# Final norm with the residual put into PSUM ahead of the last expert's rows, and a new order of low-row counts among the experts

## The chip, the cores and the metric

The kernel runs on one core of one Trainium2 chip. Five engines work side by side, each through its own queue of instructions: TensorE (PE, matrix products into PSUM), VectorE (DVE), ScalarE (ACT), GpSimd (POOL, also the issuer of gathers and scatters) and SyncE (SP, the issuer of plain DMA). They meet at semaphores. The metric is the device time of one execution in microseconds, the median of several runs.

## The reference

One decoder layer on 1024 tokens of width 1024: token mixers, cross-attention, then a hierarchical mixture of experts and a final norm. The change touches the last two.

```python
# per token: best of 4 groups, best 2 of that group's 4 experts, weights `combine` (n, 16)
a = einsum("nd,edf->nef", hf, w_gate);  b = einsum("nd,edf->nef", hf, w_up)
u = silu(a) * b * combine[..., None]
y = einsum("nef,efd->nd", u, w_down)
x = x + y
out = x * rsqrt(mean(x * x, -1) + 1e-6) * norm_final_g
```

## The kernel before

**The experts.** Each of the 16 experts gets its routed tokens as slots: 128 slots in a first part (h = 0) and, where it has more tokens, a second part of low rows (h = 1). Experts 0 and 1 run early. The other 14 are sorted by token count at run time, and `RANKS` says which rank runs at which place, so it fixes how many low rows a place has room for: ranks 0 to 3 have 64, ranks 4 to 9 have 32, ranks 10 to 13 none. Places are numbered by e = 2 to 15; e = 15 is `LAST` and has no low rows. In the loop over e the rows of expert e+1 are gathered (`fetch`, L1294, GpSimd), transposed (`turn`, L1240 for the 128 rows, L1304 for low rows), expert e's gate and up products run (`early`, L141 to L143, three passes hi·hi, hi·lo, lo·hi), then `store_low(e)` (L1376), `gate_up_low(e+1)` (L1359), and `store(e, 0)`: `down` in two halves of 512 columns, scaled on ScalarE into `yt` (L1323) and added to the rows of `xo_dram` by an indirect DMA from GpSimd (L1341). An addition waits for all additions of the expert before; within one expert the low one is issued first.

**The end.** `xo_dram` then holds the residual with all experts but `LAST`. Its eight row tiles (128 tokens by 1024) come back as `x3[0]` to `x3[7]` by eight loads on SP (L1530), which wait for expert 14's additions. `last_rows` runs `down` for `LAST`; each half is split into a high and a low part (`yl[0]` on ScalarE, L133, `yl[1]` on VectorE, L137). `mine` holds, for each row tile, a 128 by 128 selection matrix; two products with it (hi and lo) for each half put `LAST`'s rows at their tokens ("selection products"). For a tile in `ON_PE` (1, 3, 5, 7) a PSUM tile of two banks gets the selection products and then the residual, by a product of `ident` with `x3[t]` (L1565). For the others `last_add` lets VectorE add PSUM to `x3[t]` half by half (L1552). ScalarE squares and sums a tile (L1566 or L1570), takes the root (L1572), VectorE makes the factor `r` by four small instructions (L1573 to L1576). Then the tile is scaled: by VectorE from PSUM with `gfin` in one pass (L1581), or GpSimd has multiplied `x3[t]` with `gfin` (L1571) and ScalarE (L1585) or VectorE (tile 6, L1583) applies `r`. SP stores the tile (L1586).

The order of the instructions in each queue is made ahead of time by a scheduler from the order in the code and its own costs; on the chip each queue runs as it was written.

Of the kernel before, what the change touches and what calls it, by code (L numbers as in the profile page):

```python
# [12 lines left out]
AF = mybir.ActivationFunctionType  # L13
OP = mybir.AluOpType
AX = mybir.AxisListType

P = 128
D = 1024
T = 1024
KD = 8  # L20
NT = 8
# [7 lines left out]
SLOTS = 2 * P  # L29
LOW = 64  # L30
EARLY = 2
ON_PE = (1, 3, 5, 7,)
ON_V = (6,)
YTS = 2
XTS = 2
QT = 2
# [2 lines left out]
SQP = (1, 3, 5, 7)  # L39
LAST = NE - 1  # L40
NS = NE - EARLY
RANKS = [0, 10, 1, 11, 2, 12, 3, 4, 5, 6, 7, 8, 9, 13]
R64, R32 = 4, 10
DR = 0
LOWS = {EARLY + i: LOW if r < R64 else LOW // 2 if r < R32 else 0 for i, r in enumerate(RANKS)}
# [9 lines left out]
def half(n):  # L55
    return slice(n * HALF, n * HALF + HALF)


def blk(i):
    return slice(i * P, i * P + P)  # L60
# [3 lines left out]
def layer_kernel(ctx, tc, a, out, dbg=None):  # L64
    nc = tc.nc
    dbg = dbg or {}
    V, A, G, TE = nc.vector, nc.scalar, nc.gpsimd, nc.tensor
# [18 lines left out]
    @contextmanager  # L86
    def psum(**tags):
        with tc.tile_pool(name="psum", bufs=1, space=bass.MemoryType.PSUM, reuse_waits="tile") as p:
            banks.update(pool=p, tags=tags)
            yield  # L90

    def bank(tag, shape=None):
        return banks["pool"].tile(shape or [P, HALF], F32, name="ps_" + tag, tag=tag, bufs=banks["tags"][tag])

    pstack = ctx.enter_context(ExitStack())
# [7 lines left out]
    ident = consts.tile([P, P], F32, name="ident")  # L103
# [95 lines left out]
    r = hpool.tile([P, T], F32, name="r")  # L199
# [1040 lines left out]
                TE.transpose(pt[:, k], xg[:, blk(4 * b + k)], ident)  # L1240
            split(hi[:, 4 * b:4 * b + 4], lo[:, 4 * b:4 * b + 4], pt)

    def down(u_, dn, evac):
        for n in range(2):
            ps = bank("lin")
            for f in range(2):
                mm3(ps, (u_[0][:, f], u_[1][:, f]), (dn[0][f][:, half(n)], dn[1][f][:, half(n)]),
                    f == 0, f == 1)
            evac(half(n), ps)
# [282 lines left out]
    def last_rows():  # L1532

        idf = ro.tile([P, NT], F32, name="idf", tag="idf", bufs=1)
        mine = xt_p.tile([P, T], F32R, name="mine", tag="xt1b", bufs=2)
        for t in range(NT):
            V.tensor_scalar(idf[:, t:t + 1], sids[:, 0, LAST:NE], float(-t * P), None, op0=OP.add)
            V.tensor_scalar(mine[:, blk(t)], place[:, :P], idf[:, t:t + 1], None, op0=OP.is_equal)
        yl = [hxp.tile([P, D], F32R, name=f"yl{i}", tag=f"h2{i}", bufs=4) for i in range(2)]

        def evac(ns, ps):
            split(yl[0][:, ns], yl[1][:, ns], ps, scale=slots_of(LAST, 0)[:, 0, LAST:NE])

        down(U[LAST, 0], W[LAST][1], evac)
        return mine, yl

    def last_add(t):
        for n in range(2):
            ps = bank("lin")
            for i in range(2):  # L1550
                TE.matmul(ps, mine[:, blk(t)], yl[i][:, half(n)], start=i == 0, stop=i == 1)
            V.tensor_tensor(x3[t][:, half(n)], x3[t][:, half(n)], ps, op=OP.add)  # L1552

    room = [(wst, "w_hi"), (wst, "w_lo"), (wst, "w_raw"), (exg, "xg")]

    def row_sums(t):

        ss, v, r, tmp = (ro.tile([P, 1], F32, name="f" + c, tag="f" + c + "1", bufs=3) for c in "svrt")
        o = room[t // 2][0].tile([P, D], F32, name="of", tag=room[t // 2][1], bufs=2)
        if t in ON_PE:  # L1560
            x = bank("pair", [P, D])
            for n in range(2):
                for i in range(2):
                    TE.matmul(x[:, half(n)], mine[:, blk(t)], yl[i][:, half(n)], start=i == 0, stop=False)
                TE.matmul(x[:, half(n)], ident, x3[t][:, half(n)], start=False, stop=True)  # L1565
            A.activation(o, x, AF.Square, scale=0.5 * D ** -0.5, accum_out=ss)  # L1566
        else:
            last_add(t)
            x = ex.tile([P, D], F32, name="sq", tag="yt", bufs=YTS)
            A.activation(x, x3[t], AF.Square, scale=0.5 * D ** -0.5, accum_out=ss)  # L1570
            G.tensor_tensor(o, x3[t], gfin, op=OP.mult)  # L1571
        A.activation(r, ss, AF.Sqrt, bias=eps4)  # L1572
        V.tensor_scalar(v, ss, EPS / 4, None, op0=OP.add)  # L1573
        V.reciprocal(tmp, r)
        V.tensor_scalar(tmp, v, tmp, r, op0=OP.mult, op1=OP.add)
        V.reciprocal(r, tmp)  # L1576
        return t, o, x, r

    def row_out(t, o, x, r):
        if t in ON_PE:  # L1580
            V.scalar_tensor_tensor(o, x, r, gfin, op0=OP.mult, op1=OP.mult)  # L1581
        elif t in ON_V:
            V.tensor_scalar(o, o, r, None, op0=OP.mult)  # L1583
        else:
            A.activation(o, o, AF.Copy, scale=r)  # L1585
        nc.sync.dma_start(out[blk(t)], o)  # L1586

    early(LAST, 0)
# [1 line left out]
    with tc.issue_after(order["split"].ins):  # L1590
        A.activation(warm, eps, AF.Sqrt)
    pstack.close()
    pstack.enter_context(psum(lin=2, pair=3))
    mine, yl = last_rows()
    pend = []
    for t in range(NT):
        pend.append(row_sums(t))
        if t >= 1:
            row_out(*pend.pop(0))
    for x in pend:  # L1600
# [5 lines left out]
    pstack.close()  # L1606
    nover = nc.values_load(cnt[0:1, 0:1], min_val=0, max_val=T)
    with tc.If(nover > 0), psum(lin=2, tra=2, acc=1, pair=1):
        for t in ON_PE:
            last_add(t)  # L1610
        with tc.tile_pool(name="ov", bufs=1) as op_:
            with tc.For_i(0, NE, 1) as e:
                more = nc.values_load(excess[0:1, bass.ds(e, 1)], min_val=0, max_val=T)
                with tc.If(more > 0):
                    gu = gu_weights(a["w_gu"][bass.ds(e, 1)].rearrange("o p k n -> p (o k) n"),
                                    lambda i, b: op_.tile([P, 2, HALF], F32R, name=f"gu2{i}", tag=f"gu2{i}", bufs=4))
                    dn = dn_weights(a["w_dn"][bass.ds(e, 1)].rearrange("o p k n -> p (o k) n"))
                    ow = op_.tile([P, NT], F32, name="ow2")
                    nc.sync.dma_start(ow, ov_dram[:, bass.ds(e, 1)].rearrange("p o t -> p (o t)"))
                    xh = [op_.tile([P, KD, P], F32R, name=f"xh{i}") for i in range(2)]  # L1620
                    uo = [op_.tile([P, 2, P], F32R, name=f"uo{i}") for i in range(2)]
                    for t in range(NT):
                        xg = op_.tile([P, D], F32, name="xg2", tag="xg2", bufs=2)
                        nc.sync.dma_start(xg, h3_dram[blk(t)])
                        rows_in(xg, *xh)

                        def evac(ns, ps, t=t):
                            V.scalar_tensor_tensor(x3[t][:, ns], ps, ow[:, t:t + 1], x3[t][:, ns],
                                                   op0=OP.mult, op1=OP.add)

                        gate_up_t(op_, *xh, gu, *uo)
                        down(uo, dn, evac)
        with tc.tile_pool(name="fin2", bufs=1) as fn:
            for t in range(0, NT, 2):
                scaled(*sums(fn, t, 2))
# [77 lines left out]
```

## Time and profile before

| | us |
|---|---|
| median of 3 runs (1232.41 to 1239.38) | 1232.83 |
| the profiled execution | 1231.35 |
| its span, first to last instruction | 1229.5 |
| start of the residual loads | 1201.07 |
| first square of the final norm | 1208.02 |
| end of the last VectorE pass of the final norm | 1223.63 |

TensorE is busy 94% of the span, VectorE 68%, ScalarE 51%, GpSimd 33%; the granted TensorE clock is 0.988 in the mean. The times of the rows count from the span's start; what lies around the span is 1231.35 - 1229.5 = 1.85 us. In the page and the trace, "idle before" names what ended an engine's wait.

### The profile page before, as it was taken

The numbers are of one execution on the slowest core, as the hardware profiler recorded it, in microseconds if no ns is written. First come the engines' busy times: TensorE is split into PE (matmuls) and PEld (weight loads), VectorE is DVE, ScalarE is ACT, GpSimd is POOL, SyncE is SP. The second block draws the span as 40 slices with busy tenths as digits, with TensorE's granted clock in tenths as the row PEclk, the third lists the DMA queues.
The fourth block names the chain that finished last, engine by engine and source line by source line (L and its number), as shares of the span: only waits on it lengthen the run. The fifth ranks groups of instructions, "written<-read, shape, count | busy, mean of one in ns | idle before, by whom it ended". The sixth has DMA issues, their size and how long they took to land. (4 is left out here: it accounts for less than half of the span.)

```text
span 1229.5 us, 17120 instructions
## 1 busy us (share of the span) xinstructions
PE 1158.4 (94%) x6173; PEld 908.2 (74%) x6174; DVE 840.8 (68%) x1569; ACT 629.5 (51%) x1059; POOL 403.2 (33%) x276
## 2 busy tenths in 40 slices
PE   7999999999999999999999999999997798999995
PEld 3778887778877777788888787787764676667773
DVE  5499997653978788791235853655988885766665
ACT  6345564521655555482333343643752575767765
POOL 4328995301010110101011665264015122233343
PEclk9999999999999999999999999999998899999999
DMA  5211224126211111111344443244257889999967
GB/s 208 76 47 40 75 80 167 40 86 231 71 59 41 45 58 47 39 46 54 103 149 142 154 158 112 66 121 122 78 196 249 282 243 303 311 284 314 314 170 285
DMA packets 57468, 174.12 MB, mean 142 GB/s; under 512 B 7993, under 2 KB 11081, under 8 KB 57377
## 3 DMA queue, kind: packets, MB, share of 16 engines
q1 hardware_dynamic: 49680, 149.76, 36.1%
q0 software_dynamic: 7696, 23.20, 8.0%
q8 instruction: 51, 0.84, 0.3%
q14 instruction: 41, 0.33, 0.1%
HBM read 136.92 MB, written 36.01 MB: 141 GB/s over the span
## 5 line engine op out<-in xcount | busy, mean ns | idle before, releaser
L135 POOL TENSOR_TENSOR w_lo<-w_raw,w_hi 128x1024 fp32r<-128x1024 f32 x58 | 140.2, 2417 | 474.7 <-ACT w_hi L133 464.9
L143 PE MATMUL ps_lin<-hh,w_lo 128*128 128x512 f32 x560 | 222.5, 397 | 2.3 <-POOL w_lo L135 2.2
L141 PE MATMUL ps_lin<-hh,w_hi 128*128 128x512 f32 x560 | 222.9, 398 | 0.7 <-DVE u L355 0.6
L142 PE MATMUL ps_lin<-hl,w_hi 128*128 128x512 f32 x560 | 221.7, 396 | 0.0
L133 ACT ACTIVATE w_hi<-w_raw 128x1024 fp32r<-128x1024 f32 (+1 forms) x100 | 92.1, 921 | 201.2 <-PE ps_lin L142 161.0
L143 PEld LDWEIGHTS ps_lin<-hh,w_lo 128*128 128x128 f32 x560 | 105.6, 189 | 25.0 <-POOL w_lo L135 4.4
L141 PEld LDWEIGHTS ps_lin<-hh,w_hi 128*128 128x128 f32 x560 | 105.7, 189 | 23.6 <-issue 3.4
L142 PEld LDWEIGHTS ps_lin<-hl,w_hi 128*128 128x128 f32 x560 | 105.6, 189 | 21.3 <-issue 1.3
L377 DVE SCALAR_TENSOR_TENSOR ps_cva<-u,dw_w,ps_cva 128x1024 f32<-128x1024 f32 x90 | 111.6, 1279 | 0.5
L137 DVE SCALAR_TENSOR_TENSOR gu<-e_raw,gu 128x1024 fp32r<-128x1024 f32 x64 | 77.5, 1222 | 4.7 <-ACT gu L133 1.0
L373 POOL TENSOR_TENSOR oc<-oc,pj 128x512 f32<-128x512 f32 x60 | 76.0, 1323 | 8.8 <-ACT pj L372 8.7
L133 ACT ACTIVATE gu<-e_raw 128x1024 fp32r<-128x1024 f32 x64 | 67.4, 1058 | 8.9 <-PE ps_lin L143 7.4
L141 PE MATMUL ps_lin<-gu,xgT 128*128 128x512 f32 x144 | 58.3, 405 | 4.1 <-ACT xgT L133 4.1
L372 ACT ACTIVATE pj<-u,dw_w 128x512 f32<-128x512 f32 x60 | 42.4, 721 | 34.3 <-POOL oc L373 34.2
L137 DVE SCALAR_TENSOR_TENSOR dn<-d_raw,dn 128x1024 fp32r<-128x1024 f32 x32 | 39.1, 1227 | 27.8 <-ACT dn L133 27.7
L557 ACT ACTIVATE sc<-sc,mns 128x128 f32<-128x128 f32 (+3 forms) x64 | 49.4, 773 | 15.6 <-DVE mns L553 15.2
L142 PE MATMUL ps_lin<-gu,xgT 128*128 128x512 f32 x144 | 56.9, 395 | 0.0
L143 PE MATMUL ps_lin<-gu,xgT 128*128 128x512 f32 x144 | 56.6, 393 | 0.0
L1294 POOL DMA_INDIRECT xg<-h_dram,ids x29 | 34.3, 1183 | 66.2 <-PE ps_sco L1070 23.3
L137 DVE SCALAR_TENSOR_TENSOR pl<-ps_tra,ph 128x512 fp32r<-128x512 f32 (+1 forms) x80 | 49.1, 636 | 9.3 <-ACT ph L133 8.2
L133 ACT ACTIVATE ph<-ps_tra 128x512 fp32r<-128x512 f32 (+1 forms) x80 | 41.7, 552 | 23.3 <-PE ps_tra L570 22.5
L570 PE MATMUL ps_tra<-ident,sc 128*128 128x128 f32 x288 | 47.5, 274 | 4.2 <-DVE sc L560 4.2
(471 smaller groups left out, 2850.4 us busy)
## 6 DMA issues: line engine op xcount, KB each, us to landing
e_raw<-in_w_gu SPq DMA_DIRECT2D x64, 512.0 KB, 6.8
w_raw<-in_w_in SPq DMA_DIRECT2D x36, 512.0 KB, 3.8
d_raw<-in_w_dn SPq DMA_DIRECT2D x32, 512.0 KB, 9.5
w_raw<-in_w_out SPq DMA_DIRECT2D x16, 512.0 KB, 3.5
xT<-in_xT SPq DMA_DIRECT2D x16, 256.0 KB, 5.4
gc_dram<-gc SPq DMA_DIRECT2D x8, 512.0 KB, 4.2
gc<-gc_dram SPq DMA_DIRECT2D x8, 512.0 KB, 4.0
mc_dram<-gc SPq DMA_DIRECT2D x8, 512.0 KB, 2.9
```

Of the source, the lines that this page charges most:

```text
L133: order["split"] = A.activation(hi, src, AF.Copy, scale=scale)
L135: G.tensor_tensor(lo, src, hi.bitcast(F32), op=OP.subtract)
L137: V.scalar_tensor_tensor(lo, src, scale, hi.bitcast(F32), op0=OP.mult, op1=OP.subtract)
L141: TE.matmul(ps, lh, rh, start=first, stop=False)
L142: TE.matmul(ps, lh, rl, start=False, stop=False)
L143: return TE.matmul(ps, ll, rh, start=False, stop=last)
L372: A.activation(pj, uj, AF.Copy, scale=dw_h[:, c, j:j + 1])
L373: G.tensor_tensor(co[c][:, ns], co[c][:, ns], pj, op=OP.add)
L377: V.scalar_tensor_tensor(sums, u[c][:, j:j + T], dw_h[:, c, j:j + 1], sums, op0=OP.mult, op1=OP.add)
L557: A.activation(sc[:, :nk], sc[:, :nk], AF.Exp, scale=-1.0, bias=mns[:, nch - 1:nch], accum_out=sm)
L570: TE.transpose(pt[:, s_], pr[i][:, blk(j)], ident)
L1294: G.indirect_dma_start(out=XG[e, h][:n], out_offset=None, in_=src, in_offset=bass.IndirectOffsetOnAxis(ap=idx, axis=0))
```

## The change

It has two parts. In the final norm, seven of the eight tiles are now summed in PSUM (all but tile 2, `BY_ADD`), in a ring of four two-bank tiles that also holds `LAST`'s `down`. `residual(t)` puts `ident` times `x3[t]` into the tile first, two tiles ahead of the selection products. Tiles 1 and 4 (`BY_ACT`) are scaled with `r` by ScalarE out of PSUM and then multiplied with `gfin` by GpSimd; tile 2 goes by GpSimd and VectorE as tile 6 did; tiles 0, 3, 5, 6 and 7 are scaled by VectorE in one pass, the last one in two halves, each stored by itself. In `RANKS`, rank 12 moves from place 7 to place 14: place 14 loses its 32 low rows, place 7 gets 64, place 8 has 32 in place of 64, and the sum of all stays (four times 64, six times 32).

```diff
-ON_PE = (1, 3, 5, 7,)
-ON_V = (6,)
+BY_ADD = (2,)
+BY_ACT = (1, 4)
-RANKS = [0, 10, 1, 11, 2, 12, 3, 4, 5, 6, 7, 8, 9, 13]
+RANKS = [0, 10, 1, 11, 2, 3, 4, 5, 6, 7, 8, 9, 12, 13]
...
-        down(U[LAST, 0], W[LAST][1], evac)
+        ps = bank("pair", [P, D])
+        down(U[LAST, 0], W[LAST][1], evac, lambda n: ps[:, half(n)])
...
+    def residual(t):
+        if t < NT:
+            SUM[t] = bank("pair", [P, D])
+            if t not in BY_ADD:
+                for n in range(2):
+                    TE.matmul(SUM[t][:, half(n)], ident, x3[t][:, half(n)], start=True, stop=False)
...
     def row_sums(t):
...
-            last_add(t)
+        if t in BY_ADD:
+            last_add(t, SUM[t])
...
+        else:
+            x = SUM[t]
+            for n in range(2):
+                last_rows_of(x[:, half(n)], t, n, False)
+            A.activation(o, x, AF.Square, scale=0.5 * D ** -0.5, accum_out=ss)
...
     def row_out(t, o, x, r):
+        if t in BY_ADD:
+            V.tensor_scalar(o, o, r, None, op0=OP.mult)
+        elif t in BY_ACT:
+            A.activation(o, x, AF.Copy, scale=r)
+            G.tensor_tensor(o, o, gfin, op=OP.mult)
+        elif t == NT - 1:
+            for n in range(2):
+                V.scalar_tensor_tensor(o[:, half(n)], x[:, half(n)], r, gfin[:, half(n)], op0=OP.mult, op1=OP.mult)
+                nc.sync.dma_start(out[blk(t), half(n)], o[:, half(n)])
+            return
+        else:
             V.scalar_tensor_tensor(o, x, r, gfin, op0=OP.mult, op1=OP.mult)
...
-    pstack.enter_context(psum(lin=2, pair=3))
+    pstack.enter_context(psum(pair=4))
     mine, yl = last_rows()
     pend = []
+    residual(0)
+    residual(1)
     for t in range(NT):
         pend.append(row_sums(t))
+        residual(t + 2)
         if t >= 1:
             row_out(*pend.pop(0))
```

TensorE at the start of the final norm, before: the end of `LAST`'s `down` (`dn`, `uh`, `ul`), then selection products (`yl`, `mine`), and the first residual (tile 1, `x3r_11254`) after five of them.

```order
L141 MATMUL ps_lin_11338<-dn0_11200,uh_11268 128x512
L142 MATMUL ps_lin_11338<-dn1_11201,uh_11268 128x512
L143 MATMUL ps_lin_11338<-dn0_11200,ul_11269 128x512
L1564 MATMUL ps_pair_11373<-yl0_11327,mine_11310 128x512
L1564 MATMUL ps_pair_11416<-yl0_11327,mine_11310 128x512
L1551 MATMUL ps_lin_11352<-yl0_11327,mine_11310 128x512
L1551 MATMUL ps_lin_11352<-yl1_11328,mine_11310 128x512
L1564 MATMUL ps_pair_11373<-yl1_11328,mine_11310 128x512
L1565 MATMUL ps_pair_11373<-x3r_11254,ident_77 128x512
```

The same place now: `ps_pair_11329` is `down`'s tile, `11346` and `11349` are tiles 0 and 1 (line numbers of rows "now" are those of the changed kernel).

```order
L143 MATMUL ps_pair_11329<-dn0_11212,ul_11269 128x512
L1566 MATMUL ps_pair_11346<-x3r_11252,ident_77 128x512 x2
L141 MATMUL ps_pair_11329<-dn0_11208,uh_11268 128x512
L142 MATMUL ps_pair_11329<-dn1_11209,uh_11268 128x512
L143 MATMUL ps_pair_11329<-dn0_11208,ul_11269 128x512
L141 MATMUL ps_pair_11329<-dn0_11212,uh_11268 128x512
L142 MATMUL ps_pair_11329<-dn1_11213,uh_11268 128x512
L143 MATMUL ps_pair_11329<-dn0_11212,ul_11269 128x512
L1566 MATMUL ps_pair_11349<-x3r_11254,ident_77 128x512 x2
L1550 MATMUL ps_pair_11346<-yl0_11327,mine_11310 128x512
L1550 MATMUL ps_pair_11346<-yl1_11328,mine_11310 128x512
```

The residual of tile 0, which reads the loaded `x3r_11252`, now stands between the two halves of `down`, that of tile 1 behind the second half, and all selection products behind both.

VectorE at the first two tiles, before (`fs`, `fr` and `ft` are the sums, the factor `r` and a help tile; L1576 writes `r`):

```order
L1574 RECIPROCAL ft_11350<-fr_11349 128x1
L1573 TENSOR_SCALAR fv_11369<-fs_11368 128x1
L1574 RECIPROCAL ft_11371<-fr_11370 128x1
L1575 TENSOR_SCALAR ft_11350<-fv_11348,ft_11350,fr_11349 128x1
L1575 TENSOR_SCALAR ft_11371<-fv_11369,ft_11371,fr_11370 128x1
L1576 RECIPROCAL fr_11349<-ft_11350 128x1
L1576 RECIPROCAL fr_11370<-ft_11371 128x1
L1581 SCALAR_TENSOR_TENSOR of_11372<-ps_pair_11373,fr_11370,gfin_11248 128x1024
```

The same place now (L1586 writes `r`; `11354` belongs to tile 0, `11370` to tile 1, `x3r_11256` is tile 2):

```order
L1584 RECIPROCAL ft_11355<-fr_11354 128x1
L1585 TENSOR_SCALAR ft_11355<-fv_11353,ft_11355,fr_11354 128x1
L1584 RECIPROCAL ft_11371<-fr_11370 128x1
L1586 RECIPROCAL fr_11354<-ft_11355 128x1
L1585 TENSOR_SCALAR ft_11371<-fv_11369,ft_11371,fr_11370 128x1
L1601 SCALAR_TENSOR_TENSOR of_11356<-ps_pair_11346,fr_11354,gfin_11248 128x1024
L1586 RECIPROCAL fr_11370<-ft_11371 128x1
L1555 TENSOR_TENSOR x3r_11256<-x3r_11256,ps_pair_11367 128x512 x2
```

The pass of tile 0 (L1601, 1024 columns) now stands ahead of tile 1's `r`, and the two additions of tile 2 behind both.

ScalarE from the first square on, now (L1581 and L1575 square, L1582 roots, L1593 scales tile 1 from PSUM):

```order
L1581 ACTIVATE of_11356,fs_11352<-ps_pair_11346 128x1024
L1581 ACTIVATE of_11372,fs_11368<-ps_pair_11349 128x1024
L1582 ACTIVATE fr_11354<-fs_11352,eps4_11250 128x1
L1582 ACTIVATE fr_11370<-fs_11368,eps4_11250 128x1
L1593 ACTIVATE of_11372<-ps_pair_11349,fr_11370 128x1024
L1575 ACTIVATE sq_11399,fs_11388<-x3r_11256 128x1024
L1581 ACTIVATE of_11417,fs_11413<-ps_pair_11383 128x1024
```

ScalarE's scaling of tile 1 stands ahead of the squares of tiles 2 and 3.

## Rows read from the trace of the kernel before

**Rows 1.** Busy time by stretch, the final norm and what follows (columns: first line)

```profile
core 0: us, PE busy (x) PEld busy (x) DVE busy (x) ACT busy (x) POOL busy (x), PEclk, DMA share, GB/s
...
1205.70:1223.60 17.90, 13.35 (x43) 7.95 (x43) 14.39 (x45) 13.23 (x27) 9.56 (x4) 0.99 0.88 352
...
1223.60:1229.50 5.90, 0.00 (x0) 0.00 (x0) 0.04 (x1) 0.00 (x0) 0.00 (x0) 0.50 0.39 157
```

**Rows 2.** Waits of the SP queue from 1150; the residual loads, line L1530

```profile
SPq L1530 <- DMA xo_dram<-yt,sids: 35.3, 1, 35.3
...
L1530 SPq DMA_DIRECT2D x3r<-xo_dram x8: 331/384/402, 1201.1 to 1204.4; - x8
...
DMA to landing us min/median/max: 3.3/7.3/10.0
```

**Rows 3.** Timeline of TensorE (start, duration, instruction, idle before and its releaser)

```profile
1200.58 0.50 PE L141 MATMUL ps_lin<-dn,uh 128*128 128x512 f32 x1 [0.47 <-ACT uh L133]
...
1203.22 0.39 PE L143 MATMUL ps_lin<-dn,ul 128*128 128x512 f32 x1
...
1205.68 1.12 PE L1565 MATMUL ps_pair<-x3r,ident 128*128 128x512 f32 x2 [0.90 <-DMA x3r<-xo_dram]
...
1206.24 1.03 PE L1551 MATMUL ps_lin<-yl,mine 128*128 128x512 f32 x2
...
1209.35 0.39 PE L1564 MATMUL ps_pair<-yl,mine 128*128 128x512 f32 x1
...
1212.68 0.62 PE L1564 MATMUL ps_pair<-yl,mine 128*128 128x512 f32 x2
```

**Rows 4.** Timeline of ScalarE, then of VectorE, in the same stretch

```profile
1202.28 0.69 ACT L133 ACTIVATE yl<-ps_lin,wsl 128x512 fp32r<-128x512 f32 x1 [0.24 <-PE ps_lin L143]
...
1208.02 1.06 ACT L1570 ACTIVATE sq<-x3r 128x1024 f32<-128x1024 f32 x1 [3.69 <-DVE x3r L1552]
...
1204.37 0.75 DVE L137 SCALAR_TENSOR_TENSOR yl<-ps_lin,wsl,yl 128x512 fp32r<-128x512 f32 x1 [0.62 <-ACT yl L133]
...
1205.04 0.68 DVE L1552 TENSOR_TENSOR x3r<-x3r,ps_lin 128x512 f32<-128x512 f32 x1
...
1211.33 1.28 DVE L1581 SCALAR_TENSOR_TENSOR of<-ps_pair,fr,gfin 128x1024 f32<-128x1024 f32 x1
...
1222.35 1.28 DVE L1581 SCALAR_TENSOR_TENSOR of<-ps_pair,fr,gfin 128x1024 f32<-128x1024 f32 x1
```

**Rows 5.** Groups of instructions, 1204 to 1224: count | busy, mean ns | idle

```profile
L1571 POOL TENSOR_TENSOR of<-x3r,gfin 128x1024 f32<-128x1024 f32 x4 | 9.6, 2389 | 14.1 <-DVE x3r L1552 14.1
...
L1566 ACT ACTIVATE of<-ps_pair 128x1024 f32<-128x1024 f32 x4 | 4.0, 1003 | 0.0
...
L1585 ACT ACTIVATE of<-of,fr 128x1024 f32<-128x1024 f32 x3 | 3.4, 1136 | 0.0
...
L1583 DVE TENSOR_SCALAR of<-of,fr 128x1024 f32<-128x1024 f32 x1 | 0.8, 752 | 0.1
```

**Rows 6.** Timeline of GpSimd's queue, expert 14's two additions

```profile
1192.85 1.57 POOL L1341 DMA_INDIRECT xo_dram<-yt,sids_low  x1 [6.23 <-ACT yt L1323]
...
1194.72 1.56 POOL L1341 DMA_INDIRECT xo_dram<-yt,sids  x1 [0.30 <-issue]
```

**Rows 7.** Timeline of ScalarE, expert 14's second half of yt

```profile
1193.34 0.69 ACT L1323 ACTIVATE yt<-ps_lin,wsl 128x512 f32<-128x512 f32 x1 [0.67 <-PE ps_lin L143]
```

**Rows 8.** Timeline of TensorE, end of gate and up of expert 14

```profile
1187.91 0.39 PE L143 MATMUL ps_lin<-gu,xgT 128*128 128x512 f32 x1
...
1188.23 1.07 PE L1376 MATMUL ps_sco<-d_raw,uL 128*32 128x256 f32 x16
...
1190.30 0.48 PE L141 MATMUL ps_lin<-dn,uh 128*128 128x512 f32 x1
```

**Rows 9.** The output stores, line L1586

```profile
DMA to landing us min/median/max: 3.2/3.8/4.4
```

**Rows 10.** Waits of TensorE from 985 to 1205: total, times, longest

```profile
PE ps_tra L1240 <- DMA xg<-h_dram,ids: 6.2, 3, 4.9
```

More of the change, by code (lines that the diff above doesn't have):

```diff
@@ L1241, in rows_in, with down @@
             split(hi[:, 4 * b:4 * b + 4], lo[:, 4 * b:4 * b + 4], pt)
-    def down(u_, dn, evac):
+    def down(u_, dn, evac, dst=lambda n: bank("lin")):
         for n in range(2):
-            ps = bank("lin")
+            ps = dst(n)
             for f in range(2):
@@ L1542, in evac, with last_rows_of, last_add @@
             split(yl[0][:, ns], yl[1][:, ns], ps, scale=slots_of(LAST, 0)[:, 0, LAST:NE])
-        down(U[LAST, 0], W[LAST][1], evac)
+        ps = bank("pair", [P, D])
+        down(U[LAST, 0], W[LAST][1], evac, lambda n: ps[:, half(n)])
         return mine, yl
-    def last_add(t):
+    def last_rows_of(ps, t, n, first):
+        for i in range(2):
+            TE.matmul(ps, mine[:, blk(t)], yl[i][:, half(n)], start=first and i == 0, stop=i == 1)
+    def last_add(t, ps):
         for n in range(2):
[L1549 to L1552, printed above, removed]
+            last_rows_of(ps[:, half(n)], t, n, True)
+            V.tensor_tensor(x3[t][:, half(n)], x3[t][:, half(n)], ps[:, half(n)], op=OP.add)
     room = [(wst, "w_hi"), (wst, "w_lo"), (wst, "w_raw"), (exg, "xg")]
+    SUM = {}
+    def residual(t):
[4 more added lines that the diff above has]
+                    TE.matmul(SUM[t][:, half(n)], ident, x3[t][:, half(n)], start=True, stop=False)
     def row_sums(t):
@@ L1559, in row_sums @@
         o = room[t // 2][0].tile([P, D], F32, name="of", tag=room[t // 2][1], bufs=2)
[L1560 to L1567, printed above, removed]
-            last_add(t)
+        if t in BY_ADD:
+            last_add(t, SUM[t])
             x = ex.tile([P, D], F32, name="sq", tag="yt", bufs=YTS)
@@ L1579, in row_out @@
     def row_out(t, o, x, r):
-        if t in ON_PE:
+        if t in BY_ADD:
[9 more added lines that the diff above has]
+        else:
             V.scalar_tensor_tensor(o, x, r, gfin, op0=OP.mult, op1=OP.mult)
[L1582 to L1585, printed above, removed]
         nc.sync.dma_start(out[blk(t)], o)
@@ L1608, in layer_kernel @@
     with tc.If(nover > 0), psum(lin=2, tra=2, acc=1, pair=1):
-        for t in ON_PE:
-            last_add(t)
+        for t in range(NT):
+            if t not in BY_ADD:
+                last_add(t, bank("pair", [P, D]))
         with tc.tile_pool(name="ov", bufs=1) as op_:
```

## Prediction

> **What bounds the kernel now.** TensorE is busy 94% of the span, but the change works where that no longer holds, so I read the end by stretches first. In the final norm, 1205.7 to 1223.6, TensorE is busy 13.35 of 17.9 us, VectorE 14.39, ScalarE 13.23, and the DMA engines 88% [rows 1]. No engine is full; what counts is the order in which they wait for each other. After 1223.6 nothing computes: 5.9 us for the last store and the end of the program.
>
> Second, what starts the stretch. The SP queue waits for expert 14's additions and issues the eight loads of `x3` from 1201.07 on; the quickest takes 3.3 us, the last issued (1204.4) cannot take more than 10.0, so the tiles land from about 1204.4 to 1214.4 [rows 2]. TensorE has finished `LAST`'s `down` by then (12 products from 1200.58, the last started at 1203.22, so 0.23 us apiece) and first meets a load at the residual of tile 1, where it stands 0.90 us [rows 3]. The first square begins at 1208.02, the last VectorE pass ends at 1222.35 + 1.28 = 1223.63 [rows 4].
>
> So the load of `x3[0]` is the gate. VectorE read that tile at 1205.04 [rows 4], and 1201.07 + 3.3 = 1204.4 is the earliest; I take 1204.4. Today everything that waits for no load runs ahead of it: all of `down`, both splits, five selection products. What was left from 1204.4 to 1223.63 is 19.2 us.
>
> **The change, part by part: the norm.** I walk the new order from 1204.4, with durations of before.
>
> 1. TensorE now has the residual of tile 0 between the two halves of `down`. Its price: from 1209.35 to 1212.68 before, TensorE ran the two residual halves of tile 3 with its last three selection products, and tile 4's four [rows 3]. 3.33 - 7 x 0.23 = 1.72, so 0.86 per half and 1.72 per tile. It ends at 1206.1.
> 2. The second half of `down` follows, 6 x 0.23 = 1.4: 1207.5. (It also waits for VectorE's split of the first half, because both halves now lie in one tile; the ScalarE split began at 1202.28 and took 0.69 [rows 4], VectorE's takes 0.75, so this is over long before.)
> 3. The residual of tile 1, 1.72: 1209.2. Under it ScalarE and VectorE split the second half (0.69 + 0.75 from 1207.6: 1209.05), so the split costs nothing; without the cover it would cost 1.4.
> 4. Four selection products of tile 0 and their drain, 0.92 + 0.15: first square at 1210.3. Before: 1208.02.
> 5. Two squares, two roots, the four small VectorE steps. Before, from the first square to the scaling pass: 1208.02 to 1211.33, 3.3 us [rows 4]; now tile 1's `r` is not in between, so 3.1: the pass of tile 0 starts at 1213.4 and ends, after 1.28, at 1214.7.
> 6. Only then does VectorE make tile 1's `r` (0.15), and ScalarE's next instruction is the scaling of tile 1 with that `r`. Behind it in ScalarE's queue stand the squares of tiles 2 and 3, and the square of tile 2 also needs two VectorE additions that stand behind the pass. From the roots (about 1212.8) to 1214.85 ScalarE waits, some 2 us. Scaling from PSUM has no row; squaring from PSUM takes 1.003, scaling from SBUF 1.136 [rows 5]. I take 1.05: 1215.9.
> 7. GpSimd multiplies tile 1 by `gfin`, then makes tile 2's product; 2.389 each [rows 5]: 1220.7. VectorE's scaling of tile 2 waits for the second, 0.75 [rows 5]: 1221.4. Tile 3's `r` and pass stand behind it in VectorE's queue: 0.15 + 1.28, 1222.85.
> 8. Tile 7's residual needs the PSUM tile that this pass frees (a ring of four: `down`, 0, 1, 2, then 3 in `down`'s place, ..., 7 in tile 3's). In TensorE's queue it stands ahead of tile 6's selection products. 1.72 + 1.07: 1225.65. Tiles 4 and 5 and GpSimd's third product run beside this.
> 9. Squares of 6 and 7 to the pass of tile 6, as in step 5, 3.1; the pass, 1.28: 1230.0. Tile 7's `r` and two half passes, 0.15 + 2 x 0.68 (a VectorE addition of 512 columns took 0.68 [rows 4]): 1231.5.
>
> That is 27.1 us in place of 19.2: +7.9. What is saved, one ScalarE scaling (1.14) and three of the four tiles of VectorE additions (six of 0.68), lies beside this chain.
>
> The last store is half as large. 256 KB less at the stretch's 352 GB/s is 0.7 us; the bounds are nothing and 0.75. I take 0.7: +7.2.
>
> **The change: the order of low rows.** Expert 14's additions were two, issued at 1192.85 and 1194.72 [rows 6]; the first goes. The second needs `yt`, whose second half ends at 1193.34 + 0.69 = 1194.03 [rows 7], so it can gain 0.7 at most. Against that, `store_low(14)`, 1.07 us on TensorE, stood between the end of gate and up (1187.91) and `down` (1190.30) [rows 8] and covered the way from there through silu to `uh`. Without it eight transposes (1.0) remain as cover, and TensorE waits for up to 0.9 us. The addition and so the loads move by -0.7 to +0.2; I take 0. Place 7 gets 64 low rows and place 8 loses 32, the sum over all places stays, so I take 0 for the loop too.
>
> At one place of this walk everything hangs on TensorE not passing a product that waits. The trace shows it: VectorE's split ended at 1204.37 + 0.75 = 1205.12, but the selection products of tile 0 that needed only it are recorded at 1206.24, behind the residual that waited until 1205.68 [rows 3, 4]. The Trainium skill ("PSUM — Partial Sum Buffer", section "Engine vs sequencer instructions") says that matmuls start and complete in program order and that the queues of the other three engines are strict first-in first-out. If products could pass, steps 1 and 3 would leave the path and the sum would be 3.4 lower, +3.8; the trace agrees with the rule.
>
> For the half store the Trainium skill ("DMA: Bandwidth & Descriptors", section "Anatomy of one DMA — SWDGE (gpsimd) path") gives a fit of about 2.0 us plus bytes over 436 GB/s for another way of issuing. By it 512 KB take 3.2, which is the shortest of the eight stores here [rows 9], and 256 KB an estimated 2.6; the sum would be +7.3.
>
> **The rivals.**
>
> *Shorter: the residuals lie in time that TensorE had idle.* If `x3[0]` and `x3[1]` landed before the first half of `down` is through (1200.58 + 1.4 = 1202.0), steps 1 to 4 would cost little, and with one scaling less on ScalarE (1.14), half a store (0.7) and half a pass (0.64) the end would come 2.5 earlier: 1230.3. For it: TensorE does stand idle there. Against it: the loads would have to land 2.4 us earlier and the removed addition gives 0.7 at most; and steps 6 to 8 stay.
>
> *Half the loss.* Steps 6 to 8 hold 10.9 us, in which waits of three engines follow each other without a gap in my walk. If GpSimd's product or ScalarE's scaling is quicker than I take them, or the loads come 0.7 earlier, the sum falls by some 3 to 5: 1236.
>
> *More: the loop loses too.* Gathers of `xg` stand behind a low addition in GpSimd's queue, and that waits for all additions of the expert before. TensorE waited 6.2 us for gathered rows in three places, 4.9 in one [rows 10]. A second run of 64 low rows behind a first (places 6 and 7) could make one more such wait: +4.9, 1245. Against it: with 32 rows, six such places in a row cost the other two waits only, 1.3 us.
>
> **How the numbers follow.** The sum is made against the profiled execution: span 1229.5 + 7.2 = 1236.7, time 1231.35 + 7.2 = 1238.55. The median of the runs is 1232.83, 1.5 above it; on it the same sum gives 1240.0, the predicted time. Chances: the walk as it stands, 1237 to 1243, 0.66; half the loss, 0.15; more, 0.10; shorter, 0.07; anything else 0.02. The range 1235 to 1245 takes in the first, most of the second and half of the third; it leaves out the shorter one. About 1% (12.3 us) is what a measurement of this kernel can tell from no change: slower by more needs 1245.2, half of the third case, 0.06; faster by more has no case, 0.01; within 1%, 0.93.
>
> **What would show it.** Right: TensorE waits for a load behind six products of `down`; the first square about 2.3 us later; ScalarE idle for about 2 us before it scales tile 1; two GpSimd products back to back, and VectorE's tile 2 waiting for the second; the last VectorE pass near 1231.5. Wrong: a first square by 1208.5, loads issued by 1199, or a TensorE wait for `xg` at place 7 or 8.

## The result, and the profile after

The changed kernel takes 1246.4 us (median of 9 runs, 1238.69 to 1247.81) where the kernel before, over 9 runs of its own, takes 1236.46 (1232.41 to 1240.13): a ratio of 1.0076 with an interval of 1.0059 to 1.0092, so 7.3 to 11.4 us slower. The forecast was 1240.0 in a range of 1235 to 1245. The direction was right and the size was not: the range was left by 1.4 us.

| | before | changed |
|---|---|---|
| median of the runs, us | 1236.46 (the first three runs: 1232.83) | 1246.4 |
| span of the profiled execution, us | 1229.5 | 1244.4 |
| first product of `LAST`'s `down` to the end of the last VectorE pass, us | 23.05 | 30.91 |
| that end to the end of the span, us | 5.87 | 5.56 |

The two spans differ by 14.9 us, which is more than the medians do (9.9). Of the 14.9, 3.9 lie ahead of expert 13's low `down` products, 3.4 in a stretch of lower clock behind a wait at the end of the expert loop, and 7.9 in the norm; the last store gives 0.3 back. The experiments below take up each.

First the final norm. Timeline of TensorE in the changed kernel (start, duration, instruction, idle time before and its releaser), the rows that answer to [rows 3]:

```profile
1209.20 0.39 PE L143 MATMUL ps_pair<-dn,ul 128*128 128x512 f32 x1
1211.18 1.98 PE L1566 MATMUL ps_pair<-x3r,ident 128*128 128x512 f32 x4 [1.60 <-DMA x3r<-xo_dram]
1212.60 0.79 PE L141 MATMUL ps_pair<-dn,uh 128*128 128x512 f32 x1
...
1214.38 1.88 PE L1566 MATMUL ps_pair<-x3r,ident 128*128 128x512 f32 x4
1215.70 2.39 PE L1550 MATMUL ps_pair<-yl,mine 128*128 128x512 f32 x8
...
1229.88 1.95 PE L1566 MATMUL ps_pair<-x3r,ident 128*128 128x512 f32 x4 [0.49 <-PE ps_pair L1550]
```

TensorE has done the sixth product of `down` and stands 1.60 us for `x3[0]`; the other six wait behind that residual, and the residual of tile 1 stands ahead of the selection products of tile 0. Each residual has four records, two for each half. ScalarE, GpSimd and VectorE in the same stretch, which answer to [rows 4, 5]:

```profile
1217.22 1.02 ACT L1581 ACTIVATE of<-ps_pair 128x1024 f32<-128x1024 f32 x1 [1.95 <-PE ps_pair L1550]
...
1221.71 1.11 ACT L1593 ACTIVATE of<-ps_pair,fr 128x1024 f32<-128x1024 f32 x1 [2.01 <-DVE fr L1586]
...
1222.91 2.36 POOL L1594 TENSOR_TENSOR of<-of,gfin 128x1024 f32<-128x1024 f32 x1 [20.11 <-ACT of L1593]
1225.23 2.37 POOL L1576 TENSOR_TENSOR of<-x3r,gfin 128x1024 f32<-128x1024 f32 x1
...
1210.34 0.75 DVE L137 SCALAR_TENSOR_TENSOR yl<-ps_pair,wsl,yl 128x512 fp32r<-128x512 f32 x1 [2.01 <-ACT yl L133]
...
1220.33 1.28 DVE L1601 SCALAR_TENSOR_TENSOR of<-ps_pair,fr,gfin 128x1024 f32<-128x1024 f32 x1
...
1227.64 0.75 DVE L1591 TENSOR_SCALAR of<-of,fr 128x1024 f32<-128x1024 f32 x1 [0.41 <-POOL of L1576]
...
1228.50 1.28 DVE L1601 SCALAR_TENSOR_TENSOR of<-ps_pair,fr,gfin 128x1024 f32<-128x1024 f32 x1
...
1237.43 1.41 DVE L1597 SCALAR_TENSOR_TENSOR of<-ps_pair,fr,gfin 128x512 f32<-128x512 f32 x2
```

ScalarE stands 2.01 us before it scales tile 1, GpSimd makes two products back to back, VectorE's tile 2 waits for the second. Then the end of the expert loop, which the forecast put down as worth nothing. TensorE and GpSimd there:

```profile
1192.67 1.06 PE L1240 MATMUL ps_tra<-ident,xg 128*128 128x128 f32 x8 [1.96 <-DMA xg<-h_dram,ids]
...
1194.75 0.79 PE L141 MATMUL ps_lin<-dn,uh 128*128 128x512 f32 x1 [0.80 <-ACT uh L133]
...
1186.38 1.57 POOL L1341 DMA_INDIRECT xo_dram<-yt,sids_low  x1 [8.87 <-DVE dn L137]
1188.26 1.00 POOL L1294 DMA_INDIRECT xg<-h_dram,ids  x1 [0.30 <-PE ps_lin L143]
...
1201.23 1.57 POOL L1341 DMA_INDIRECT xo_dram<-yt,sids  x1 [9.78 <-ACT yt L1323]
```

The last gather of `xg` is issued at 1188.26, behind expert 13's low addition, and TensorE stands 1.96 us for its rows and another 0.80 for `uh`. Neither wait is there before. Busy time by stretch, with the granted clock in the third column from the end:

```profile
core 0: us, PE busy (x) PEld busy (x) DVE busy (x) ACT busy (x) POOL busy (x), PEclk, DMA share, GB/s
...
1195.00:1200.00 5.00, 5.00 (x12) 3.87 (x13) 1.76 (x8) 0.69 (x1) 0.00 (x0) 0.50 0.09 17
...
1211.18:1238.84 27.66, 21.53 (x66) 12.21 (x66) 14.12 (x42) 13.00 (x27) 7.09 (x3) 0.99 0.62 249
1238.84:1244.40 5.56, 0.00 (x0) 0.00 (x0) 0.00 (x1) 0.00 (x0) 0.00 (x0) 0.50 0.38 144
```

Behind those waits the granted clock is 0.50, that is 1.2 of 2.4 GHz, from about 1194 to 1201. The norm has grown to 27.66 us, 21.53 of them with TensorE busy; in [rows 1] it was 13.35 of 17.9.

### The profile page after: what moved, and what is told of

It reads as the page before. It is cut to its first block, busy times and chain, and to the rows that moved or that the text cites. A ratio compares the mean times of both kernels' runs of the same rounds, so it can differ in the third digit from the quotient of the medians.

```text
span 1244.4 us, 17142 instructions
## 1 busy us (share of the span) xinstructions
PE 1170.1 (94%) x6185; PEld 914.2 (73%) x6186; DVE 839.7 (67%) x1565; ACT 628.4 (50%) x1058; POOL 402.6 (32%) x275
```

## The experiments

All kernels compute the whole result. The table holds four stretches of every profiled execution; a ratio is of several runs, with its interval, and three rows are of a single execution. S is the start of expert 13's low `down` products (L1376), D the first product of `LAST`'s `down`, V the end of the last VectorE pass; each is read from the timelines as above (before: S is 1174.31, D and V are 1200.58 and 1222.35 + 1.28 in [rows 3, 4]).

| kernel | start to S | S to D | D to V | V to end | ratio to before |
|---|---|---|---|---|---|
| before | 1174.31 | 26.27 | 23.05 | 5.87 | |
| before, again | 1174.58 | 26.30 | 22.49 | 5.83 | one execution |
| old norm, new order (`ranks_only`) | 1181.93 | 26.06 | 22.76 | 5.75 | 1.0037 (1.0008 to 1.0065) |
| new norm, old order (`norm_only`) | 1178.34 | 26.28 | 30.80 | 5.38 | 1.0060 (1.0037 to 1.0083) |
| changed | 1178.23 | 29.70 | 30.91 | 5.56 | 1.0076 (1.0059 to 1.0092) |
| changed, again | 1183.10 | 26.30 | 30.66 | 5.64 | one execution |
| changed, whole last store | 1183.02 | 31.60 | 30.21 | 5.87 | one execution |
| residuals behind `down` | 1175.71 | 26.10 | 28.09 | 5.50 | 1.0039 (1.0014 to 1.0065) |
| the same, old order | 1175.88 | 26.27 | 28.47 | 5.48 | 1.0025 (0.9995 to 1.0054) |
| the same, new order, no ScalarE scaling | 1181.28 | 26.08 | 28.32 | 5.42 | 1.0064 (1.0037 to 1.0090) |
| changed, unread rows gone | 1174.85 | 23.51 | 33.95 | 5.49 | 1.0048 (1.0018 to 1.0078) |
| before, unread rows gone | 1179.41 | 25.38 | 22.69 | 6.02 | 0.9979 (0.9953 to 1.0005) |
| before, expert 13 without low rows | none | | 22.62 | 5.64 | 0.9998 (0.9970 to 1.0026) |
| before, unread rows gone, last store halved | 1173.95 | 25.41 | 22.82 | 5.52 | 0.9997 (0.9969 to 1.0026) |

### The two parts of the change, each alone

The theory was that the norm's queue order is the whole loss; the rival, that the new order of low rows costs part of it.

```diff
 # norm_only: the changed kernel, and
-RANKS = [0, 10, 1, 11, 2, 3, 4, 5, 6, 7, 8, 9, 12, 13]
+RANKS = [0, 10, 1, 11, 2, 12, 3, 4, 5, 6, 7, 8, 9, 13]
 # ranks_only: the kernel before, and
-RANKS = [0, 10, 1, 11, 2, 12, 3, 4, 5, 6, 7, 8, 9, 13]
+RANKS = [0, 10, 1, 11, 2, 3, 4, 5, 6, 7, 8, 9, 12, 13]
```

> The changed norm with the order of low rows of before. Theory (the loss is the norm's queue order): the tail from the landing of the first x3 tile to the last VectorE pass stays 27.7 us as in the changed kernel (19.3 before), the last store ends 0.3 sooner, so about +8.0 us on the kernel before, ratio 1.0065. Rival (the new order of low rows costs part of what was measured): ratio 1.005 or less, with the rest in the run that changes only that order. Second rival (what the profile of the changed kernel shows before 1000 us, 7.1 us later than before in lines that did not change, belongs to the change): the gather at 993 us in before is again 3 us or more late here.

> The kernel before with the new order of low rows alone. Theory: it is worth nothing within 0.1%, ratio 0.9990 to 1.0010; the second addition of expert 14 is issued within 1 us of where it was relative to the start of the expert loop, and the tail stays 19.3 us. Rival (the loop loses): TensorE waits one more time for xg at place 7 or 8, up to 4.9 us, ratio up to 1.004. Rival (the removed addition gives the loads of x3 a lead): ratio 0.9994.

The norm alone gives 1.0060, which is 7.4 us, and a D to V of 30.80: the theory's number. The interval, 1.0037 to 1.0083, does not by itself exclude the rival's 1.005. But the order alone gives 1.0037, or 4.6 us with bounds of 1.0 and 8.0, where the theory allowed 1.0010 at most; the lower bound, 1.0008, just touches that. So the theory falls in its second half, though the size of the order's part is uncertain. The two parts add up to 12.0 us, 2.6 more than both together cost by the ratio of the changed kernel; the intervals allow for it. TensorE in the profile of the kernel with the new order alone:

```profile
1181.93 1.07 PE L1376 MATMUL ps_sco<-d_raw,uL 128*32 128x256 f32 x16
...
1195.44 1.06 PE L1240 MATMUL ps_tra<-ident,xg 128*128 128x128 f32 x8 [1.52 <-DMA xg<-h_dram,ids]
...
1197.52 0.50 PE L141 MATMUL ps_lin<-dn,uh 128*128 128x512 f32 x1 [0.80 <-ACT uh L133]
...
1207.99 0.50 PE L141 MATMUL ps_lin<-dn,uh 128*128 128x512 f32 x1 [0.47 <-ACT uh L133]
```

The same two waits as in the changed kernel, with the old norm: they belong to the order. The products that stood there before are seen in the kernel with the new norm and the old order:

```profile
1179.23 0.60 PE L1359 MATMUL ps_sco<-e_raw,xgL 128*32 128x128 f32 x10
...
1180.17 1.73 PE L1359 MATMUL ps_sco<-e_raw,xgL 128*32 128x128 f32 x54
...
1192.27 1.07 PE L1376 MATMUL ps_sco<-d_raw,uL 128*32 128x256 f32 x16
```

Expert 14's 32 low rows are 64 records for gate and up and 16 for `down` (32 and 8 products in the code, each with two records), some 3.2 us on TensorE between S and D. Without them S to D is 26.06 to 26.30 (four executions with the new order) in place of 26.27 to 26.30 (four with the old): 3.2 us of work were taken out and 0.2 or less came back. Most of the rest is waiting: 1.52 to 1.75 us for the last gather, which stands behind expert 13's low addition in GpSimd's queue (and that addition waits for the additions before it), 0.80 and 0.23 for `uh`. In two more executions with the new order the granted clock fell to 0.50 behind that wait, and S to D took 29.70 and 31.60. The 32 rows were not saved either: they are now done at places 7 and 8.

The 3.2 us are not the price, though. From VectorE's first product of expert 2's low rows (L1362), near the start of the loop, to V, profiles that differ in the order alone and have much the same wait for `xg` early in the loop lie close together: 220.81 us with the new order (1009.94 to 1230.75 in `ranks_only`, early wait 4.6) against 219.84 before (1003.79 to 1223.63, 4.9), and 221.44 against 220.19 for the kernels with the residuals behind `down`, described next (0.5 and 0.6). So 1.0 and 1.3 us of the order's cost stand in like profiles; whether what the runs show above that is the lower clock and the waits that some executions have, or the spread of the runs, is not shown.

The second rival of the first text, that the lateness before the loop belongs to the change, is taken up further below.

### Residuals behind `down`

Steps 1 and 3 of the prediction say that TensorE's order costs 3.4 us at the start of the norm. Here the residual of tile 0 follows all of `down`, and tile 1's follows the selection products of tile 0. The two halves of `down` also get a PSUM tile each, so that the second no longer waits for VectorE's split of the first.

```diff
...
-        ps = bank("pair", [P, D])
-        down(U[LAST, 0], W[LAST][1], evac, lambda n: ps[:, half(n)])
+        down(U[LAST, 0], W[LAST][1], evac, lambda n: bank("pair", [P, D])[:, half(0)])
...
-    residual(0)
-    residual(1)
+    with tc.issue_after(order["down"].ins):      # the last product of down
+        residual(0)
     for t in range(NT):
         pend.append(row_sums(t))
+        if t == 0:
+            with tc.issue_after(order["sel"].ins):   # tile 0's last selection product
+                residual(1)
         residual(t + 2)
```

> The changed kernel with tile 0's residual put behind all of LAST's down (whose halves get a PSUM tile each, so that the second half does not wait for VectorE's split) and tile 1's residual behind tile 0's selection products. Theory (steps 1 to 3 of the prediction, 3.4 us of TensorE's order, are on the path): the first square comes 2.9 us after the landing of x3[0] in place of 6.0, and the end 2.6 earlier than in the changed kernel (0.8 of it is lost again behind VectorE, which waits for tile 2's additions): tail 25.0, ratio 1.0044. Rival (TensorE's order is hidden and only the links ScalarE, GpSimd, VectorE count): the first square comes earlier but the last pass does not, tail 27.7, ratio 1.0065.

Its TensorE, ScalarE and VectorE:

```profile
1204.45 0.39 PE L143 MATMUL ps_pair<-dn,ul 128*128 128x512 f32 x1
1204.87 1.98 PE L1565 MATMUL ps_pair<-x3r,ident 128*128 128x512 f32 x4
1206.29 1.48 PE L1549 MATMUL ps_pair<-yl,mine 128*128 128x512 f32 x4
...
1207.81 1.02 ACT L1580 ACTIVATE of<-ps_pair 128x1024 f32<-128x1024 f32 x1 [2.25 <-PE ps_pair L1549]
...
1214.14 0.69 DVE L1554 TENSOR_TENSOR x3r<-x3r,ps_pair 128x512 f32<-128x512 f32 x1 [0.82 <-PE ps_pair L1549]
...
1228.49 1.41 DVE L1596 SCALAR_TENSOR_TENSOR of<-ps_pair,fr,gfin 128x512 f32<-128x512 f32 x2
```

The first square comes 2.94 us behind the first residual (6.04 in the changed kernel, 1211.18 to 1217.22), and from that residual to V it is 25.03, where 25.0 was expected and the changed kernel has 27.66. The order of TensorE's queue, with the separate PSUM tiles, is worth 2.6 us at the end; 0.5 of the 3.1 at the start is lost again further on. How much each of the two is worth was not run apart: in the changed kernel VectorE's split of the first half ended at 1210.34 + 0.75 = 1211.09, only 0.09 ahead of the residual, so in the shared tile the second half of `down` could hardly have started ahead of it. The ratio is 1.0039.

> The run with the residuals behind down, with the old order of low rows. Theory (the new order costs 1.8 us at the end of the loop): from the transposes before the last gather to LAST's first down product 18.8 us in place of 20.6, tail 25.0 as there, ratio 1.0025 where the new order gave 1.0039. Rival (the order of low rows is worth nothing): 1.004.

With the old order of low rows it is 1.0025 and S to D is 26.27. The two orders now stand against each other three times, with 4.6 us (old norm), 2.0 (1.0076 against 1.0060) and 1.7 (1.0039 against 1.0025) for the new one, each a difference that single intervals do not exclude from zero but for the first.

### No scaling on ScalarE

Steps 6 and 7 are a chain over ScalarE and GpSimd, some 7 us with its second product. Does the kernel with the residuals behind `down` get them back if the chain goes?

```diff
-BY_ACT = (1, 4)
+BY_ACT = ()
```

> The same, and no tile is scaled on ScalarE: tiles 1 and 4 are scaled by VectorE passes, and GpSimd has tile 2's product alone. Theory that the steps 6 and 7 hold 7 us that this would give back at once: tail 20 to 21, ratio near 1.000. What I expect instead from a walk with the measured durations: VectorE gets two passes more (2 x 1.28) and is late for tile 2's additions and for every later tile, so that the end stays within 0.5 of the run without it, tail 25.2, ratio 1.0045.

It does not. VectorE in this kernel:

```profile
1218.08 1.28 DVE L1600 SCALAR_TENSOR_TENSOR of<-ps_pair,fr,gfin 128x1024 f32<-128x1024 f32 x1
1219.28 0.68 DVE L1554 TENSOR_TENSOR x3r<-x3r,ps_pair 128x512 f32<-128x512 f32 x1
1220.78 0.69 DVE L1554 TENSOR_TENSOR x3r<-x3r,ps_pair 128x512 f32<-128x512 f32 x1 [0.83 <-PE ps_pair L1549]
...
1234.27 1.41 DVE L1596 SCALAR_TENSOR_TENSOR of<-ps_pair,fr,gfin 128x512 f32<-128x512 f32 x2
```

The pass of tile 1 (1218.08) now stands ahead of tile 2's additions, and from the first residual (1210.25) to V it takes 25.43, 0.4 more than with the chain. So the links of steps 6 and 7, which the walk has on the path of the changed kernel, have VectorE's own work right behind them; in the changed kernel itself they were not taken out. The two ratios, 1.0064 and 1.0039, do not tell these kernels apart.

### Is it the cover, or the queue? The last gather

Three kernels ask what the wait at the end of the loop is made of. In the first, expert 13 has no low rows and expert 14 keeps its 32. In the other two the gather and the eight transposes of `LAST`'s second half of slots are left away; nothing reads them. Then the last gather is issued ahead of expert 13's low addition.

```diff
 # ranks_cover (old norm)
+RANKS = [0, 10, 1, 11, 2, 3, 4, 5, 6, 7, 8, 12, 9, 13]
 # no_dead (old norm), after_no_dead (changed kernel)
-        if e + 2 <= LAST:
+        if e + 2 < LAST:
             fetch(e + 2, 1)
-        turn(e + 1, 1)
+        if e + 1 < LAST:
+            turn(e + 1, 1)
```

> The kernel before with an order of low rows in which expert 13 has none and expert 14 keeps its 32 (places 7 and 8 as in the changed kernel). Theory: what the new order costs is the cover that expert 14's low rows gave on TensorE (64 products of gate and up, 16 of down) while the last gather stood behind expert 13's low addition on GpSimd's queue. Here the cover is back and that addition is gone, so TensorE does not wait for the last gather, and from the transposes before it to LAST's first down product it takes 18.8 us or less, as with the old order (20.6 with the new one): ratio 1.0000. Rival (64 low rows at place 7 cost by themselves): 18.8 there, but 2 to 3 us more from the start of the expert loop to those transposes, ratio 1.002.

> The kernel before without the gather and the eight transposes of LAST's second half of slots, which no instruction reads. Theory: TensorE saves the 1.0 us of the transposes and GpSimd a gather, the last gather moves ahead of a whole expert's additions; at most 1.0 us less, ratio 0.999 to 1.000, less than a measurement can tell. Rival: the transposes are cover too, and without them TensorE waits as long for the same uh, ratio 1.000.

> The changed kernel without that gather and those transposes, so that the last gather is issued ahead of expert 13's low addition and not behind it. Theory (the wait of 1.5 to 2.0 us comes from the gather's place in GpSimd's queue): the wait is gone, the wait of 0.8 for uh stays, and the time falls by the wait and the transposes, 2.5 us: ratio 1.0055 where the changed kernel has 1.0076. Rival (the wait belongs to the load of the memory, not to the queue): a wait for xg of 1 us or more stays at this place.

TensorE in the first:

```profile
1185.25 1.73 PE L1240 MATMUL ps_tra<-ident,xg 128*128 128x128 f32 x7 [4.49 <-DMA xg<-h_dram,ids]
...
1191.65 1.03 PE L1240 MATMUL ps_tra<-ident,xg 128*128 128x128 f32 x8
...
1210.44 0.50 PE L141 MATMUL ps_lin<-dn,uh 128*128 128x512 f32 x1 [0.47 <-ACT uh L133]
```

With the cover back there is no wait for the last gather, and from the transposes ahead of it to D it takes 18.79, as expected. But a wait of 4.49 stands at the gather before. It has moved to the expert that has no low rows now. The ratio, 0.9998, does not show this cost, so how much of it is in every execution stays open. The rival, that 64 low rows at place 7 cost by themselves, is not excluded: its 1.002 lies inside the interval of 0.9970 to 1.0026.

In the kernel before, leaving out the unread rows shortens S to D by 0.9 us, to 25.38, about as expected; the ratio of 0.9979 cannot be told from 1. GpSimd, VectorE and TensorE in the changed kernel without the unread rows:

```profile
1185.57 1.95 POOL L1341 DMA_INDIRECT xo_dram<-yt,sids  x1 [0.31 <-issue]
1192.96 1.55 POOL L1341 DMA_INDIRECT xo_dram<-yt,sids  x1 [5.44 <-DMA xo_dram<-yt,sids]
...
1200.78 0.75 DVE L137 SCALAR_TENSOR_TENSOR yl<-ps_pair,wsl,yl 128x512 fp32r<-128x512 f32 x1 [2.02 <-ACT yl L133]
...
1202.81 3.17 PE L1567 MATMUL ps_pair<-x3r,ident 128*128 128x512 f32 x4 [2.79 <-DMA x3r<-xo_dram]
1204.99 1.42 PE L141 MATMUL ps_pair<-dn,uh 128*128 128x512 f32 x1
```

The wait of 1.5 to 2.0 us is gone: the place in GpSimd's queue made it. S to D falls to 23.51, by 2.6 to 2.8 against the four executions with the new order at full clock (2.5 was expected). But D to V rises to 33.95. TensorE is early and the loads of `x3` are not: expert 14's addition is issued at 1192.96, when the addition before it has landed, and `x3[0]` is there 9.8 us after that (9.4 to 10.0 in the six profiles in which TensorE waits for it). TensorE stands 2.79 us, and the four records of the residual then take 3.17 in place of 1.98, at the lower clock. In this profile all of the gain is given back. The runs do not settle whether that holds in every execution: their 1.0048 is near the 1.0055 that was expected, and the interval of 1.0018 to 1.0078 takes in the changed kernel's 1.0076 too. At the end of the loop it is the row of additions on GpSimd, one waiting for the landing of the last, that TensorE's work must cover.

### The profile that the prediction was made from

Up to the start of the loop the profiles of the changed kernel lay 7 us behind that of before, in lines that are the same. Here each kernel is profiled once more, and the changed kernel once with a whole last store:

```diff
 # whole_store: the changed kernel without
-        elif t == NT - 1:
-            for n in range(2):
-                V.scalar_tensor_tensor(o[:, half(n)], x[:, half(n)], r, gfin[:, half(n)], ...)
-                nc.sync.dma_start(out[blk(t), half(n)], o[:, half(n)])
-            return
```

> The kernel before once more, one look. Theory: the profiled execution that the prediction was made from was 5 us ahead of the usual before anything that the change touches; here the start of the expert loop comes 4 to 7 us later than there, as in the eight other profiles, and the time is nearer 1236 than 1231. Rival (the shift belongs to the changed kernels): within 1 us of the first profile there.

> The changed kernel once more, one look. Theory: the tail is 27.7 us again and the wait of 1.5 to 2.0 us for the last gather is there again, but TensorE's fall to half its clock behind that wait (3.6 us in the first profile) is chance: from expert 13's low down products to LAST's down 26.1 us as in three other kernels with the new order. Rival: the fall comes with this kernel, 29.7 again.

> The changed kernel with its last tile scaled by one pass and stored whole, as before; one look. Theory: the last pass ends 0.1 earlier, and the end comes 5.8 us behind it in place of 5.5. By the prediction's term it would be 0.7 later.

The second profile of the kernel before has its first product of expert 2's low rows (VectorE, L1362) 4.1 us later than in the first profile, 1007.86 against 1003.79. The changed kernel's two profiles have it 7.2 and 6.7 later, and the kernels with the old norm 4.1 to 7.5. So most of this shift is not the change. The expected time near 1236 was wrong: the execution took 1230.97, and its span is 1229.2, because another wait is missing. TensorE's waits from 985 to 1205 in it (total, times, longest), which answer to [rows 10]:

```profile
PE ps_acc L1271 <- DVE uu L1268: 2.9, 2, 2.0
...
PE ps_tra L1240 <- DMA xg<-h_dram,ids: 0.4, 2, 0.2
```

The 4.9 us for gathered rows in [rows 10] are gone in the same kernel. A wait of 4.0 to 4.9 us for `xg`, ending between 1035 and 1042, is there in one of six profiles with the old order and in four of the seven with the new one that changed nothing else there. GpSimd's queue is the same up to that place, so I take it as chance, but that is not shown: seven and six are too few. This column of the table ("start to S") tells nothing about the change.

The changed kernel's second profile has S to D of 26.30 and a wait of 1.75, without the lower clock. With the whole last store the lower clock is back, behind a longer wait, and the execution took 1252.47 us, more than any of the nine of the changed kernel; only its last stretch is used here:

```profile
1198.54 1.94 PE L1240 MATMUL ps_tra<-ident,xg 128*128 128x128 f32 x8 [3.53 <-DMA xg<-h_dram,ids]
...
1201.44 0.79 PE L141 MATMUL ps_lin<-dn,uh 128*128 128x512 f32 x1 [0.53 <-ACT uh L133]
```

From V to the end it is 5.87, as before. The eight profiles with halves have 5.38 to 5.64, mean 5.50; the six with a whole store 5.64 to 6.02, mean 5.83. The halves are worth 0.3, and their two passes take 1.41 in place of 1.28.

### A version that beats both?

> The kernel before without the gather and transposes of LAST's unread second half, and with the last tile scaled and stored by halves (of the change this part alone). Theory: 0.9979 was measured for the first part; the halves take 0.3 to 0.5 us off the time from the last VectorE pass to the end (5.9 before, 5.4 to 5.6 in the runs with halves), less 0.1 for the second pass: ratio 0.9976. Rival: the 0.9979 was chance (its bounds are 0.9953 and 1.0005), then 0.9995 or more.

The kernel before without the unread rows had 0.9979. With the last store halved on top it has 0.9997 (0.9969 to 1.0026), which speaks for chance in the first number, though the two intervals overlap; both profiles keep the 0.9 us between S and D. No version here is measurably faster than the kernel before.

## Why the prediction was wrong

Its range was left by three terms. The largest is none of the change's.

**The base.** The sum was put on the median of three runs, 1232.83. Nine runs give 1236.46, and the three larger sets of runs of the same kernel 1236.57, 1236.55 and 1234.80. The base was 3.6 us low by the nine, and the spread of those three (1232.41 to 1239.38) had said that it could be. The profile's own time, 1231.35, is lower still.

**The order of low rows, taken as 0.** This is the step that failed: "The addition and so the loads move by -0.7 to +0.2; I take 0. [...] so I take 0 for the loop too." The step counted the cover that expert 14's low `down` products gave on the way to `uh` and foresaw that wait (up to 0.9; 0.80 came). It did not follow the other queue: expert 14's products for gate and up also covered GpSimd's additions, behind which the last gather stands. Measured: TensorE stands 1.5 to 2.0 us for the last gather (3.5 once), and the new order costs 4.6, 2.0 and 1.7 us in three comparisons of runs, mean 2.8, of which like profiles show 1.0 and 1.3. How the rest comes about stays open: a lower clock behind that wait (in two of six executions) and the early wait for `xg` would make it up if they come more often with the new order. The rival "the loop loses too" had the right kind of wait, for `xg`, but at places 7 and 8, where no profile has one, and with a chance of 0.10 only.

**The last store, taken as -0.7.** Measured: -0.3 in the time after the last pass. By the fit of the Trainium skill ("DMA: Bandwidth & Descriptors", section "Anatomy of one DMA — SWDGE (gpsimd) path"), given there for another way of issuing, it would be an estimated 0.6 for the half; the runs show half of that, and the measurement decides.

**The norm, +7.9: right.** D to V is 30.91, 30.66 and 30.80 with the new norm and 23.05, 22.49 and 22.76 with the old: +8.0. The walk held step by step. That the predicted D to V, 1231.5 - 1200.58 = 30.9, was met so closely is in part luck: `x3[0]` came 3.25 us behind D (1207.93 to 1211.18) where the walk had 3.82, and the steps took 27.7 in place of 27.1.

| steps | predicted | measured in the changed kernel |
|---|---|---|
| 1, 2: residual 0 and the second half of `down` | 3.12 | 3.20 (1211.18 to 1214.38) |
| 3, 4: residual 1, selection products, first square | 2.79 | 2.84 (to 1217.22) |
| 5: two squares to the end of tile 0's pass | 4.38 | 4.39 (1220.33 + 1.28) |
| 6: `r` of tile 1, ScalarE's scaling | 1.20 | 1.21 (1221.71 + 1.11) |
| 7: GpSimd twice, VectorE's tile 2, pass of tile 3 | 6.96 | 6.96 (1228.50 + 1.28) |
| 8: residual 7, rows of 6 | 2.79 | 3.02 (first square of tile 6 at 1232.80) |
| 9: to the last pass | 5.89 | 6.04 (1237.43 + 1.41) |
| sum | 27.1 | 27.7 |

The scaling from PSUM, which had no row, took 1.11 where 1.05 was taken. Ahead of residual 7 TensorE stood 0.49 us, until 0.10 behind the end of tile 3's pass (1229.78), whose PSUM tile it needs; the profile names a TensorE product as the releaser. That matmuls stay in their order is seen again, most clearly without the unread rows: VectorE's split was over at 1200.78 + 0.75 = 1201.53, but the six products of `down` that needed no load started only at 1204.99, behind the residual that waited until 1202.81. This agrees with the Trainium skill ("PSUM — Partial Sum Buffer", section "Engine vs sequencer instructions"), by which matmuls start in program order. Taking the residuals from ahead of those products, together with a PSUM tile for each half, gave 2.6 us, where steps 1 and 3 together had been priced at 3.4.

The sum with the measured terms: 1236.5 + 8.0 - 0.3 + 2.8 = 1247.0, against 1246.4 measured. It is not an independent check, because one of the three comparisons behind the 2.8 uses the changed kernel's own time.

Of the rivals, "shorter" and "half the loss" are out: `x3[0]` landed after the first half of `down`, not before it, and no link of steps 6 to 8 was quicker by more than 0.03 us. What stays open: how often the granted clock falls behind the wait for the last gather (in two of six executions with the new order and that wait), and whether the long wait for `xg` early in the loop comes more often with the new order.

## What to carry to other kernels

Work that is taken from an engine at a place where it covered another queue's chain gives its time back only down to that chain: before it is priced at its duration, follow the queue that runs beside it (here additions on GpSimd, each waiting for the landing of the last, with gathers between them). A residual put into PSUM ahead of the sum puts the load's wait ahead of everything that stands behind it in TensorE's queue; it belongs behind the work that needs no load. And a forecast of less than a per cent needs a base of more than three runs, and a second profile of the kernel before, since one profile can lack or hold a wait of 5 us by chance.

## What the runs showed of the hardware that was not expected

- A short wait can cost more than its length. After waits of 1.52 to 1.75 us for the last gather and 0.80 for `uh` TensorE went on at a granted clock of 1.00, 2.4 GHz (four executions with the new order). With a wait of 1.96 and the same 0.80 the clock was 0.50 (1.2 GHz) from the second wait on, with one of 3.53 from the first on, and S to D was 3.4 and 5.3 us over the 26.3 of the others; of the 5.3, about 1.8 is the longer wait itself.
- From the issue of expert 14's addition to the arrival of `x3[0]` it takes 9.4 to 10.0 us in the six profiles in which TensorE waits for it (1192.96 to 1202.81 and 1201.23 to 1211.18 are two), whether that wait is 0.39 or 2.79 us.
- The residual by `ident` took 0.86 us for a half of 512 columns by the rows of before and shows two records for each half, 0.43 us apart; the selection products of the same shape in fp32r start 0.23 us apart.
